# A diffusion layer on one Trainium2 core: the right-hand blocks of the second tokens made in another order, and three of them ranked lower

## The chip, the core and the metric

The kernel runs on one core of a Trainium2 chip. The metric is the device time of one execution in microseconds (us); for the kernel before it is the median of three executions, 2676.26 us (2675.55 to 2680.1). Five engines work side by side and meet through semaphores: TensorE (PE in the profile; its weight loads are PEld), VectorE (DVE), ScalarE (ACT), GpSimd (POOL) and SyncE (SP), whose queue issues most DMAs.

## The reference

The layer takes 1024 latent tokens and 256 context tokens of width 1024. Cut to what matters here:

```python
def swiglu(h, w_in, w_out):
    a, b = jnp.split(h @ w_in, 2, axis=-1)
    return (jax.nn.silu(a) * b) @ w_out
...
# 1. half-step: x += 0.5 * gate * swiglu(modulate(rms_norm(x)))       (D_FF = 2816)
# 2. mixers:    p = modulate(rms_norm(x)) @ w_in                       (1024 x 6656)
#               conv branch and attention branch from p, gated, merged, one projection
# 3. half-step: as 1, with weights of its own, then a final rms_norm
```

Everything is float32. The change touches the two large products h @ w_in of the mixers and of the second half step, and of these only the blocks made from h.

## The kernel before, in words

**Products.** The latent tokens are worked on transposed (channels on partitions), in two chunks of 512: C0, the first tokens, and C1, the second tokens. A float32 factor is held as two parts, hi (rounded to the matmul's type) and lo (the rest). `split` makes them: a cast on ACT writes hi, then a subtraction on DVE writes lo (L197). One product of a weight block with a right-hand block sums 4 k-blocks of 3 matmuls each (hi x hi, hi x lo, lo x hi; `terms`, L680), so 12 matmuls of 128x128 by 128x512 into one PSUM bank. The weight's lo part is needed by every third matmul, and so is the right-hand lo part.

**Seven products instead of eight.** The class `Winograd` takes 1024 channels as two halves and two chunks of tokens as two columns: a 2x2 block product, for which it uses seven block products. Products 1 and 2 need only the first tokens (right-hand blocks r1, r2). Products 3 to 7 need blocks made from the second tokens. With f1, f2 the two channel halves of the first tokens and b1, b2 those of the second tokens, `norm1` (L556) makes, for each k of 4 blocks of 128 channels: t1 = b1 - f1 (block 5), t2 = b2 - t1 (block 6), t3 = b2 - b1 (block 7), t2 - f2 (block 4) and b2 itself (block 3). `keep(i, k, src)` (L513) takes a buffer and splits a block into its parts. So five blocks by four k are 20 splits, and 20 rows on DVE write a lo part: these are rows r3 to r7 below.

**Weights.** Per pair of weight columns (a, b), POOL forms s1 = b0 + b1, s2 = s1 - a0, s3 = a0 - b0 and, when s2 has been split, s2 again as a1 - s2. `parts` splits these on ACT and DVE into tiles `wl` (4 buffers). `lefts` (L617) lists them in the order in which they are used: s2 (product 6), s3 (product 7), b1 (product 4, from a raw tile), s1 (product 5), the second s2 (product 3).

**Stages and order.** Product results go to 5 PSUM banks. `start(norm)` (L702) runs products 1 and 2 of the first 9 pairs, one step of `norm1` after each pair's first product, so that the second tokens' blocks are made while PE has first-token products. Sums of the third pair on are put aside to DRAM. `run(norm)` ends it. Then, pair by pair, `second` (L770) uses products 6, 7 and 4 and `third` (L780) uses 5 and 3. `mix` (the mixers, `plain=True`, 9 pairs ahead) and `fast` (the second half step, 9 pairs ahead) both call `norm1()` (started at L1301 and L1776); the first half step calls it with `turned` (L1106), which takes the tokens from elsewhere.

The program is written in one order, but a scheduler that runs when the kernel is built lays out each engine's list: it ranks instructions by their place in the program, and puts on an engine the best ranked one that it reckons can run. `tc.high_priority(n)` moves the rank of what is written under it. So the order of writing, the pools and the ranks decide together which row stands where. On the chip each engine runs its list strictly in order.

**Pools.** `apool` has 38 buffers (`atile`; r blocks, h blocks, x tiles), `tpool` 11 of one 128x512 tile (`ttile`; nt, h22, s1 to s3, u, c, v, b), `wpool` 4 for `wl` and 3 for `raw`.

Of the kernel before, what the change touches and what calls it, by code (L numbers as in the profile page):

```python
# [45 lines left out]
TOKENS_AT = 5  # L46
RESIDENT, AH2, AH3 = 2, 9, 9
SLOT = 1024


@with_exitstack
def tile_dit_layer(
# [198 lines left out]
    def rstd_cols(accs, n, dim):  # L251

        nt = n // P
        pss = ps_t(nt)
        for j in range(nt):
            for i, acc in enumerate(accs):
                matmul(
                    pss[:, j : j + 1], acc[:, j * P : (j + 1) * P], ones[:], start=(i == 0),
                    stop=(i == len(accs) - 1), pinned=True,
                )  # L260
        a = small("rs_a", nt)
        dve.tensor_scalar(out=a[:], in0=pss, scalar1=dim * EPS, scalar2=None, op0=ALU.add)
# [228 lines left out]
    class Winograd:  # L491
# [61 lines left out]
                dve.tensor_add(out=accs[0], in0=accs[0], in1=sq)  # L553
            self.n_squares[ch] = n + 1

        def norm1(self, turned=None):  # L556

            if turned is None:
                y = rstd_cols(self.accs[C1], 512, D)
                yield  # L560
                pr = bcast(y, 512)
                yield
            t12, t22 = {}, {}

            def scaled(k):
                t22[k] = ttile("h22")
# [5 lines left out]
                for t, i in ((t12[k], k), (t22[k], k + 4)):  # L572
                    if turned is not None:
                        self.shifted(t, i, turned(i))
                        continue
                    dve.tensor_mul(out=t, in0=self.xs(i, C1), in1=pr)
                    self.shifted(t, i)

            scaled(0)
            for k in range(4):  # L580
                f, b12, b22 = self.h0[k], t12[k], t22[k]
                t1, t2, t3 = ttile("nt"), ttile("nt"), ttile("nt")
                dve.tensor_sub(out=t1, in0=b12, in1=f[:, 0])
                self.keep(3, k, b22)
                dve.tensor_sub(out=t3, in0=b22, in1=b12)
                if k < 3:
                    scaled(k + 1)
                dve.tensor_sub(out=t2, in0=b22, in1=t1)
                self.keep(7, k, t3)
                self.keep(5, k, t1)  # L590
                self.keep(6, k, t2)
                dve.tensor_sub(out=t2, in0=t2, in1=f[:, 1])
                self.keep(4, k, t2)
                yield
# [1268 lines left out]
```

## Time and profile before

| | |
|---|---|
| median of three executions | 2676.26 us (2675.55 to 2680.1) |
| the profiled execution's own time | 2677.21 us |
| its span in the profile | 2675.3 us, at a mean granted clock of 0.995 |
| PE busy | 2637.8 us, 99% of the span |
| DVE busy | 2007.0 us, 75% |
| ACT, POOL busy | 1172.3 us (44%), 557.1 us (21%) |

The mixers' `start` ends near 950 us, that of the second half step near 2075 us. A page of the profile gives whole-span shares; the timeline view prints pieces of one engine with the idle time ahead of each in brackets and, behind the arrow, what ended it; the windows view gives the busy time of each engine in a stretch. All operations are recorded by one helper, so all carry line L90, and tiles tell them apart (r, wl, nt, uc with their numbers left out).

### The profile page before, as it was taken

The page shows a single profiled execution, that of the slowest core. Times are in us where ns is not written, and L with a number is a line of the kernel's source. Part 1 is how long each engine was busy: PE and PEld are TensorE (multiplying, and loading weights), DVE is VectorE, ACT ScalarE, POOL GpSimd, SP SyncE. Part 2 cuts the span into 40 slices and gives each one's busy share as a digit, 9 for nine tenths or more (in the row PEclk, how much of TensorE's full clock was granted, in tenths as well). Part 3 has the DMA queues.
Part 4 walks back from the last instruction along what each step waited for, and adds up shares of the span by engine and source line. Part 5 has one row for each costly group of instructions (what it writes and reads, how often), then busy time and mean ns, then how long its engine had stood idle before and what let it go on. Part 6 is the DMA issues. An engine that isn't in the chain of part 4 may idle for free.

```text
span 2675.3 us, 36939 instructions
## 1 busy us (share of the span) xinstructions
PE 2637.8 (99%) x13373; PEld 2222.0 (83%) x13373; DVE 2007.0 (75%) x3356; ACT 1172.3 (44%) x2317; POOL 557.1 (21%) x449
## 2 busy tenths in 40 slices
PE   8999999999999999999999999999999999999998
PEld 6787799888778878888999888888888788888888
DVE  5788976788877899877588676685458876667885
ACT  6532454333453643333355576574236333334443
POOL 0134201211010044332033122141001442320200
PEclk9999999999999999999999999999999999999999
DMA  8566475345974345332522432113524543228841
GB/s 316 196 190 191 141 227 165 108 131 197 300 188 110 114 157 173 114 126 79 201 66 94 91 95 61 35 42 99 164 87 146 181 153 93 89 87 284 189 90 64
DMA packets 369744, 376.93 MB, mean 141 GB/s; under 512 B 19334, under 2 KB 258072, under 8 KB 369560
## 3 DMA queue, kind: packets, MB, share of 16 engines
q1 hardware_dynamic: 358744, 353.03, 40.7%
q0 software_dynamic: 10816, 21.53, 4.9%
q8 instruction: 105, 1.72, 0.3%
q14 instruction: 79, 0.65, 0.1%
HBM read 306.78 MB, written 67.67 MB: 140 GB/s over the span
## 4 chain that ended last, share of the span: by engine, by line
PE 92%; DVE 4%; issue 1%; DMA 1%; ACT 1%; POOL 0%; SPq 0%; DVEq 0%; POOLq 0%; ACTq 0%
PE ps L90 76%; PE po L90 8%; PE pt L90 8%; DVE r L90 1%; DVE wl L90 1%; DVE nt L90 0%; DVE macc L90 0%; DMA rawm<-in_w_mod_dram 0%; DVE uc L90 0%; POOL s L90 0%; DMA raw<-in_ffn_w_in_dram 0%; DMA ws<-in_ffn_w_out_dram 0%; DVE v L90 0%; DVE y L90 0%; DMA mcol<-mrow 0%
## 5 line engine op out<-in xcount | busy, mean ns | idle before, releaser
L90 PE MATMUL ps<-r,wl 128*128 128x512 f32 x5196 | 1206.9, 391 | 10.6 <-DVE wl L90 5.2
L90 PEld LDWEIGHTS ps<-r,wl 128*128 128x128 f32 x5196 | 973.6, 188 | 220.1 <-DVE wl L90 7.7
L90 ACT CAST wl<-s 128x512 fp32r<-128x512 f32 x254 | 156.8, 620 | 322.2 <-PE ps L90 225.1
L90 POOL TENSOR_TENSOR s<-raw 128x512 f32<-128x512 f32 x64 | 91.9, 1436 | 891.3 <-DMA raw<-in_ffn_w_in_dram 583.5
L90 ACT CAST wl<-raw 128x512 fp32r<-128x512 f32 x287 | 177.5, 620 | 219.1 <-PE ps L90 157.6
L90 DVE TENSOR_TENSOR wl<-raw,wl 128x512 fp32r<-128x512 f32 x287 | 202.4, 706 | 62.5 <-ACT wl L90 59.7
L90 DVE TENSOR_TENSOR wl<-s,wl 128x512 fp32r<-128x512 f32 x254 | 230.7, 909 | 18.3 <-ACT wl L90 16.9
L90 POOL TENSOR_TENSOR s<-raw,s 128x512 f32<-128x512 f32 x64 | 103.9, 1624 | 363.2 <-DVE wl L90 363.2
L90 DVE SCALAR_TENSOR_TENSOR macc<-rawm,silu_c,macc 128x512 f32<-128x512 f32 x178 | 149.7, 858 | 12.5 <-DMA rawm<-in_w_mod_dram 11.7
L90 PE MATMUL ps<-wh,r 128*128 128x256 f32 x768 | 141.6, 284 | 0.0
L90 DVE TENSOR_TENSOR u<-u,ps 128x512 f32<-128x512 f32 x174 | 118.3, 680 | 29.0 <-PE ps L90 28.9
L90 DVE TENSOR_TENSOR pts<-pt,pts 128x512 fp32r<-128x512 f32 x160 | 108.7, 687 | 40.8 <-ACT pts L90 39.0
L90 ACT CAST pts<-pt 128x512 fp32r<-128x512 f32 x160 | 93.3, 595 | 86.5 <-PE pt L90 82.6
L90 ACT CAST rh<-hid 128x512 fp32r<-128x512 f32 x132 | 81.3, 620 | 109.5 <-PE ps L90 94.5
L90 DVE TENSOR_REDUCE m<-ps 128x1 f32<-128x512 f32 (+1 forms) x192 | 110.3, 595 | 24.1 <-PE ps L90 20.4
L90 PE MATMUL ps<-rh,wl 128*128 128x512 f32 x360 | 123.1, 392 | 2.8 <-ACT rh L90 2.8
L90 PEld LDWEIGHTS ps<-wh,r 128*128 128x128 f32 x768 | 120.8, 192 | 0.7 <-issue 0.6
L90 ACT CAST wh<-raw 128x512 fp32r<-128x512 f32 (+1 forms) x85 | 67.9, 801 | 102.1 <-PE ps L90 71.8
L90 PE MATMUL po<-pts,vh 128*128 128x512 f32 x256 | 110.0, 435 | 0.2 <-ACT pts L90 0.2
L90 PE MATMUL ps<-wl,r 128*128 128x256 f32 x384 | 109.0, 284 | 0.0
L90 DVE TENSOR_TENSOR rl<-hid,rh 128x512 fp32r<-128x512 f32 x132 | 90.1, 686 | 22.8 <-PE ps L90 13.4
L90 PE MATMUL ps<-kl,qs 128*128 128x512 f32 x384 | 104.2, 395 | 0.0
(314 smaller groups left out, 5117.4 us busy)
## 6 DMA issues: line engine op xcount, KB each, us to landing
raw<-in_ffn_w_in_dram SPq DMA_DIRECT2D x130, 512.0 KB
raw<-in_ffn_w_out_dram SPq DMA_DIRECT2D x72, 512.0 KB
raw<-in_w_in_dram SPq DMA_DIRECT2D x61, 512.0 KB
rawm<-in_w_mod_dram SPq DMA_DIRECT2D x104, 256.0 KB
hid<-hd SPq DMA_DIRECT2D x40, 512.0 KB
rawm<-in_w_mod_dram SPq DMA_DIRECT2D x32, 512.0 KB
ws<-in_ffn_w_out_dram POOLq DMA_DIRECT2D x30, 512.0 KB, 6.5
ucd<-uc SPq DMA_DIRECT2D x25, 512.0 KB
```

What stands on the lines that cost most here:

```text
L90: inst = getattr(self.engine, name)(*args, **kw)
```

## The change

`norm1` is written anew for the mixers and the second half step, and its old order stays as `norm1_turned` for the first half step, which is thereby unchanged. In the new `norm1` each step makes blocks 6 and 7 of its k, and only the float32 sources of blocks 5, 3 and 4. These sources stand in six `apool` buffers named `raws` (two k in one) where t1 and b2 stood in `ttile`s before. After the fourth k the blocks 4, 5 and 3 are split, four k each, all under a rank 300 lower. The operations and their number are the same: DVE has 3265 rows before and after, with 20 splits per stage.

```diff
+LATER = 300
...
+        def norm1(self):
...
+            def raw(i, k):
+                if k % 2 == 0:
+                    held[i] = atile("raws", (P, 2, 512))
+                raws[i, k] = held[i][:, k % 2]
+                return raws[i, k]
...
+                for t, i in ((t12[k], k), (raw(3, k), k + 4)):
                     dve.tensor_mul(out=t, in0=self.xs(i, C1), in1=pr)
                     self.shifted(t, i)
+
+            scaled(0)
+            for k in range(4):
+                f, b12, b22 = self.h0[k], t12[k], raws[3, k]
+                t1, t2, t3 = raw(5, k), ttile("nt"), ttile("nt")
+                dve.tensor_sub(out=t1, in0=b12, in1=f[:, 0])
+                if k < 3:
+                    scaled(k + 1)
+                dve.tensor_sub(out=t2, in0=b22, in1=t1)
+                dve.tensor_sub(out=t3, in0=b22, in1=b12)
+                self.keep(6, k, t2)
+                self.keep(7, k, t3)
+                dve.tensor_sub(out=raw(4, k), in0=t2, in1=f[:, 1])
+                if k < 3:
+                    yield
+            for i in (4, 5, 3):
+                with tc.high_priority(-LATER):
+                    for k in range(4):
+                        self.keep(i, k, raws[i, k])
+                yield
+
+        def norm1_turned(self, turned):
...
-    norm1 = half1.norm1(lambda k: turned(t1, k, ps_t if k < 4 else ps_o))
+    norm1 = half1.norm1_turned(lambda k: turned(t1, k, ps_t if k < 4 else ps_o))
```

The order of rows differs from before only around the ends of the two stages. In the rows below a name's first number counts tiles, so r4_1549 is block 4; `h22` and `nt` are the float32 sources before, `raws` those of the change; lines read L90 before and L91 after, since one line was added above.

**Mixers, DVE, before**, where the weights of the first pair's products 6, 7 and 4 (wl_1584, wl_1588, wl_1590) are split:

```order
L90 TENSOR_TENSOR nt_1541_8572<-nt_1541_8572,x1_1191_6610 128x512
L90 TENSOR_TENSOR wl_1584_8748<-s2_1582_8743,wl_1584_8748 128x512
L90 TENSOR_TENSOR r4_1549_8596<-nt_1541_8572,r4_1549_8596 128x512
L90 TENSOR_TENSOR r3_1560_8642<-h22_1544_8579,r3_1560_8642 128x512
L90 TENSOR_TENSOR r7_1561_8647<-nt_1559_8640,r7_1561_8647 128x512
L90 TENSOR_TENSOR r5_1562_8650<-nt_1557_8638,r5_1562_8650 128x512
L90 TENSOR_TENSOR r6_1563_8653<-nt_1558_8639,r6_1563_8653 128x512
L90 TENSOR_TENSOR wl_1588_8768<-s3_1583_8744,wl_1588_8768 128x512
L90 TENSOR_TENSOR wl_1590_8785<-raw_1580_8740,wl_1590_8785 128x512
```

**The same place with the change**; the weights of products 6 and 7 are wl_1582 and wl_1586 here:

```order
L91 TENSOR_TENSOR r4_1551_8622<-raws_1512_8454,r4_1551_8622 128x512
L91 TENSOR_TENSOR wl_1582_8746<-s2_1580_8741,wl_1582_8746 128x512
L91 TENSOR_TENSOR r4_1552_8625<-raws_1512_8454,r4_1552_8625 128x512
L91 TENSOR_TENSOR r4_1553_8628<-raws_1539_8569,r4_1553_8628 128x512
L91 TENSOR_TENSOR r4_1554_8631<-raws_1539_8569,r4_1554_8631 128x512
L91 TENSOR_TENSOR r5_1562_8673<-raws_1506_8437,r5_1562_8673 128x512
L91 TENSOR_TENSOR wl_1586_8766<-s3_1581_8742,wl_1586_8766 128x512
```

and further on (three more rows of r5, two of r3 and a sum stand between the two pieces) the weight of product 4, wl_1588:

```order
L91 TENSOR_TENSOR r3_1575_8730<-raws_1523_8499,r3_1575_8730 128x512
L91 TENSOR_TENSOR r3_1576_8733<-raws_1523_8499,r3_1576_8733 128x512
L91 TENSOR_TENSOR uc_1585_8765<-uc_1585_8765,ps_1589_8786 128x512
L91 TENSOR_TENSOR wl_1588_8783<-raw_1578_8738,wl_1588_8783 128x512
L91 TENSOR_TENSOR wl_1600_8813<-s1_1579_8740,wl_1600_8813 128x512
L91 TENSOR_TENSOR wl_1602_8831<-s2_1580_8741,wl_1602_8831 128x512
```

The lo part of product 6's weight moves from the 1187th row of the list to the 1182nd. That of product 4's stood 7 rows behind it and now stands 15 behind it, and eleven of the rows between are held-back blocks, r4_1552 to r3_1576.

**Mixers, PE, before**, from product 6 of the first pair on (x3 is all three matmuls of one k; x2 two matmuls on the weight's hi part):

```order
L90 MATMUL ps_1603_8818<-r6_1514_8458,wl_1584_8748 128x512 x3
L90 MATMUL ps_1603_8818<-r6_1531_8525,wl_1584_8748 128x512 x3
L90 MATMUL ps_1603_8818<-r6_1548_8592,wl_1584_8748 128x512 x3
L90 MATMUL ps_1603_8818<-r6_1563_8653,wl_1584_8748 128x512
L90 MATMUL ps_1605_8836<-r7_1512_8452,wl_1588_8768 128x512 x2
L90 MATMUL ps_1612_8863<-r4_1515_8462,wl_1590_8785 128x512 x2
L90 MATMUL ps_1603_8818<-r6_1563_8653,wl_1584_8748 128x512 x2
L90 MATMUL ps_1614_8880<-r5_1513_8455,wl_1602_8815 128x512 x2
```

**PE with the change**, from the last groups of product 7 on:

```order
L91 MATMUL ps_1603_8834<-r7_1538_8566,wl_1586_8766 128x512 x3
L91 MATMUL ps_1603_8834<-r7_1550_8618,wl_1586_8766 128x512 x3
L91 MATMUL ps_1610_8861<-r4_1551_8622,wl_1588_8783 128x512 x2
L91 MATMUL ps_1612_8878<-r5_1562_8673,wl_1600_8813 128x512 x2
L91 MATMUL ps_1614_8896<-r3_1573_8724,wl_1602_8831 128x512 x2
L91 MATMUL ps_1610_8861<-r4_1551_8622,wl_1588_8783 128x512
L91 MATMUL ps_1610_8861<-r4_1552_8625,wl_1588_8783 128x512 x3
L91 MATMUL ps_1610_8861<-r4_1553_8628,wl_1588_8783 128x512 x3
```

Products 6 and 7 run through whole. Then PE takes, of each of products 4, 5 and 3, the two matmuls on the weight's hi part, and its next one needs the lo part of wl_1588.

**Second half step, DVE, before**; the weights of products 6, 7 and 4 are wl_3619, wl_3623 and wl_3625:

```order
L90 TENSOR_TENSOR r7_3581_19451<-nt_3577_19438,r7_3581_19451 128x512
L90 TENSOR_TENSOR r5_3582_19454<-nt_3575_19436,r5_3582_19454 128x512
L90 TENSOR_TENSOR r6_3583_19457<-nt_3576_19437,r6_3583_19457 128x512
L90 TENSOR_TENSOR wl_3619_19613<-s2_3617_19608,wl_3619_19613 128x512
L90 TENSOR_TENSOR wl_3623_19633<-s3_3618_19609,wl_3623_19633 128x512
L90 TENSOR_TENSOR nt_3576_19437<-nt_3576_19437,h0_3478_18939 128x512
L90 TENSOR_TENSOR wl_3625_19650<-raw_3615_19605,wl_3625_19650 128x512
L90 TENSOR_TENSOR uc_3622_19632<-uc_3622_19632,ps_3626_19653 128x512
L90 TENSOR_TENSOR wl_3630_19671<-s1_3616_19607,wl_3630_19671 128x512
L90 TENSOR_TENSOR r4_3584_19461<-nt_3576_19437,r4_3584_19461 128x512
```

**With the change**; they are wl_3615, wl_3619 and wl_3621:

```order
L91 TENSOR_TENSOR r5_3596_19539<-raws_3539_19300,r5_3596_19539 128x512
L91 TENSOR_TENSOR uc_3603_19569<-uc_3603_19569,ps_3616_19612 128x512
L91 TENSOR_TENSOR r5_3597_19542<-raws_3566_19415,r5_3597_19542 128x512
L91 TENSOR_TENSOR r5_3598_19545<-raws_3566_19415,r5_3598_19545 128x512
L91 TENSOR_TENSOR wl_3615_19609<-s2_3613_19604,wl_3615_19609 128x512
L91 TENSOR_TENSOR wl_3619_19629<-s3_3614_19605,wl_3619_19629 128x512
L91 TENSOR_TENSOR r3_3606_19587<-raws_3538_19295,r3_3606_19587 128x512
L91 TENSOR_TENSOR wl_3621_19646<-raw_3611_19601,wl_3621_19646 128x512
L91 TENSOR_TENSOR r3_3607_19590<-raws_3538_19295,r3_3607_19590 128x512
L91 TENSOR_TENSOR uc_3618_19628<-uc_3618_19628,ps_3622_19649 128x512
L91 TENSOR_TENSOR r3_3608_19593<-raws_3556_19362,r3_3608_19593 128x512
L91 TENSOR_TENSOR wl_3626_19667<-s1_3612_19603,wl_3626_19667 128x512
```

Blocks 4 and 5 are done before the weights of product 6; product 6's lo part moves from the 2605th row to the 2609th. The last rows of block 3 stand between the weights' rows.

**Second half step, PE, before**, the end of the first pair's products:

```order
L90 MATMUL ps_3631_19674<-r6_3598_19518,wl_3619_19613 128x512 x2
L90 MATMUL ps_3640_19719<-r4_3599_19522,wl_3625_19650 128x512 x3
L90 MATMUL ps_3644_19757<-r3_3544_19306,wl_3632_19689 128x512 x3
L90 MATMUL ps_3644_19757<-r3_3561_19373,wl_3632_19689 128x512 x3
L90 MATMUL ps_3644_19757<-r3_3578_19440,wl_3632_19689 128x512 x3
L90 MATMUL ps_3644_19757<-r3_3595_19507,wl_3632_19689 128x512 x3
L90 MATMUL ps_3650_19783<-r6_3549_19323,wl_3639_19716 128x512 x2
```

**PE with the change**, the beginning of the first pair's second products:

```order
L91 MATMUL ps_3627_19670<-r6_3543_19311,wl_3615_19609 128x512 x2
L91 MATMUL ps_3629_19688<-r7_3544_19314,wl_3619_19629 128x512 x2
L91 MATMUL ps_3636_19715<-r4_3584_19485,wl_3621_19646 128x512 x2
L91 MATMUL ps_3638_19735<-r5_3595_19536,wl_3626_19667 128x512 x2
L91 MATMUL ps_3627_19670<-r6_3543_19311,wl_3615_19609 128x512
L91 MATMUL ps_3627_19670<-r6_3557_19369,wl_3615_19609 128x512 x3
```

Before, the last group of product 4 needed r4_3599, DVE's 2617th row. With the change the last row that product 3 needs is r3_3609, also the 2617th; product 6's lo part is the first that PE comes to, behind 8 matmuls on weights' hi parts.

More of the change, by code (lines that the diff above doesn't have):

```diff
@@ L554, in square @@
             self.n_squares[ch] = n + 1
[L556 to L563, printed above, removed]
+        def norm1(self):
+            y = rstd_cols(self.accs[C1], 512, D)
+            yield
+            pr = bcast(y, 512)
+            yield
+            t12, raws, held = {}, {}, {}
+            def raw(i, k):
[3 more added lines that the diff above has]
+                return raws[i, k]
             def scaled(k):
-                t22[k] = ttile("h22")
                 if self.plain:
@@ L571, in scaled @@
                     t12[k] = ttile("h12")
[L572 to L575, printed above, removed]
+                for t, i in ((t12[k], k), (raw(3, k), k + 4)):
                     dve.tensor_mul(out=t, in0=self.xs(i, C1), in1=pr)
                     self.shifted(t, i)
+            scaled(0)
[11 more added lines that the diff above has]
+                if k < 3:
+                    yield
+            for i in (4, 5, 3):
+                with tc.high_priority(-LATER):
+                    for k in range(4):
+                        self.keep(i, k, raws[i, k])
+                yield
+        def norm1_turned(self, turned):
+            t12, t22 = {}, {}
+            def scaled(k):
+                t22[k], t12[k] = ttile("h22"), ttile("h12")
+                for t, i in ((t12[k], k), (t22[k], k + 4)):
+                    self.shifted(t, i, turned(i))
             scaled(0)
```

## The prediction

> **What bounds the kernel now.** I read the page's shares and its chain first, then PE's timeline around the ends of the two stages that call `norm1`, then what DVE, POOL, SP and ACT do there. From the page, busy time by engine and the chain's shares:
>
> ```profile
> PE 2637.8 (99%) x13373; PEld 2222.0 (83%) x13373; DVE 2007.0 (75%) x3356; ACT 1172.3 (44%) x2317; POOL 557.1 (21%) x449
> ...
> PE 92%; DVE 4%; issue 1%; DMA 1%; ACT 1%; POOL 0%; SPq 0%; DVEq 0%; POOLq 0%; ACTq 0%
> ```
>
> PE is busy for 99% of the span. No matmul goes or comes, so the change can only touch what PE waits. PE's timeline (start, us, engine, group; in brackets the idle time ahead and what ended it) in the mixers, then in the second half step:
>
> ```profile
> 922.01 30.87 PE L90 MATMUL ps<-r,wl 128*128 128x512 f32 x135
> 955.67 1.89 PE L90 MATMUL ps<-r,wl 128*128 128x512 f32 x7 [2.79 <-DVE wl L90]
> 957.80 1.77 PE L90 MATMUL ps<-r,wl 128*128 128x512 f32 x5 [0.24 <-ACT r L90]
> 959.96 18.66 PE L90 MATMUL ps<-r,wl 128*128 128x512 f32 x81 [0.38 <-DVE r L90]
> ```
>
> ```profile
> 2031.29 43.73 PE L90 MATMUL ps<-r,wl 128*128 128x512 f32 x191
> 2075.24 0.73 PE L90 MATMUL ps<-r,wl 128*128 128x512 f32 x2 [0.22 <-DVE r L90]
> 2077.57 0.50 PE L90 MATMUL ps<-r,wl 128*128 128x512 f32 x1 [1.61 <-ACT r L90]
> 2078.30 4.37 PE L90 MATMUL ps<-r,wl 128*128 128x512 f32 x18 [0.23 <-DVE r L90]
> 2083.54 31.82 PE L90 MATMUL ps<-r,wl 128*128 128x512 f32 x139 [0.86 <-DVE wl L90]
> ```
>
> The waits are 2.79 + 0.24 + 0.38 = 3.41 us in the mixers and 0.22 + 1.61 + 0.23 + 0.86 = 2.92 us in the second half step, 6.33 us in all or 0.24% of the time. That is the most that a better order can give, and each of them ends on a row of DVE or of ACT that makes parts. Why they are late, the windows show (length; busy us and count of PE, PEld, DVE, ACT, POOL; granted clock; DMA share; GB/s):
>
> ```profile
> 950.00:960.00 10.00, 6.56 (x26) 4.12 (x24) 9.92 (x15) 5.37 (x10) 2.11 (x2) 1.00 0.26 96
> 2060.00:2070.00 10.00, 10.00 (x45) 8.09 (x44) 9.39 (x11) 4.79 (x10) 5.72 (x4) 1.00 0.36 120
> 2070.00:2080.00 10.00, 7.94 (x33) 5.72 (x32) 9.25 (x10) 3.71 (x7) 4.71 (x3) 1.00 0.55 186
> ```
>
> DVE is full in both places, 9.92 and 9.39 of 10 us. So DVE is the local bound: a row moved ahead there pushes others back, one for one.
>
> **The units.** A long piece of the chain gives PE's time per matmul; DVE's timeline, from a row to a later one, gives DVE's:
>
> ```profile
> 1040.37 117.11 PE ps L90 x516
> ```
>
> ```profile
> 2031.57 1.28 DVE L90 TENSOR_TENSOR h<-x,pt 128x512 f32<-128x512 f32 x2 [0.42 <-PE pt L90]
> ...
> 2059.22 0.68 DVE L90 TENSOR_TENSOR r<-h,r 128x512 fp32r<-128x512 f32 x1
> 2060.61 0.69 DVE L90 TENSOR_TENSOR uc<-uc,ps 128x512 f32<-128x512 f32 x1 [0.71 <-PE ps L90]
> 2061.22 4.06 DVE L90 TENSOR_TENSOR r<-nt,r 128x512 fp32r<-128x512 f32 x3
> 2065.20 1.28 DVE L90 TENSOR_TENSOR wl<-s,wl 128x512 fp32r<-128x512 f32 x2
> ```
>
> A matmul costs 117.11 / 516 = 0.227 us. The first and the second of these DVE rows are 46 places apart in its list, so a row costs (2059.22 - 2031.57) / 46 = 0.60 us when nothing disturbs it.
>
> **Mixers, what goes.** DVE's timeline here, with the rows on which the argument rests:
>
> ```profile
> 951.93 0.68 DVE L90 TENSOR_TENSOR nt<-h,h 128x512 f32<-128x512 f32 x1
> ...
> 954.94 0.68 DVE L90 TENSOR_TENSOR wl<-s,wl 128x512 fp32r<-128x512 f32 x1
> ...
> 958.02 1.88 DVE L90 TENSOR_TENSOR r<-nt,r 128x512 fp32r<-128x512 f32 x3
> ...
> 962.41 1.61 DVE L90 TENSOR_TENSOR r<-nt,r 128x512 fp32r<-128x512 f32 x1
> ```
>
> The row at 954.94 writes the lo part of product 6's weight and is what the 2.79 us wait ends on; it is the 1187th of DVE's list, and the row at 951.93 is the 1182nd. The new list has product 6's lo part there. It is then done by 952.6, before PE comes at 922.01 + 30.87 = 952.88, and the wait goes. The two small waits for r rows go too: blocks 6 and 7 all stand ahead.
>
> **Mixers, what comes.** Products 6 and 7 hold 24 matmuls, then PE has 2 each of products 4, 5 and 3 that use the weight's hi part only: 30 in all, until 952.88 + 30 x 0.227 = 959.7. Next it needs the lo part of product 4's weight, which now stands 15 rows behind that of product 6. Fifteen rows from 951.93 on end at 962.41 in the trace, so this part would start there and be written by 963.1: **a wait of 3.4 us**. The 15 rows at 0.60 us would take only 9.0 and leave 1.9. More is possible, because POOL moves ahead as well. POOL's timeline, and SP's queue:
>
> ```profile
> 955.70 1.85 POOL L90 TENSOR_TENSOR s<-raw,s 128x512 f32<-128x512 f32 x1 [5.44 <-DVE wl L90]
> 961.33 2.13 POOL L90 TENSOR_TENSOR s<-raw 128x512 f32<-128x512 f32 x1 [3.78 <-DMA raw<-in_w_in_dram]
> ...
> 2058.63 2.43 POOL L90 TENSOR_TENSOR s<-raw 128x512 f32<-128x512 f32 x1 [202.95 <-DMA raw<-in_ffn_w_in_dram]
> 2061.14 1.29 POOL L90 TENSOR_TENSOR s<-s,raw 128x512 f32<-128x512 f32 x1
> 2062.39 1.74 POOL L90 TENSOR_TENSOR s<-raw,raw 128x512 f32<-128x512 f32 x1
> ```
>
> ```profile
> 957.58 3.94 SPq L90 DMA_DIRECT2D raw<-in_w_in_dram  x2
> ```
>
> POOL's last operation of the pair waits for the very lo part that moves ahead by 5 rows, 3 us. It ends at 957.55, SP issues the next pair's load at 957.58 and POOL's next three operations begin at 961.33. With the change that burst begins near 959 (3.0 us earlier would be 958.3; the load's landing may not follow wholly) and lies on the 15 rows for about 4 us. What a burst costs, the second half step shows: the three r rows at 2061.22 took 4.06 us, and the three at 958.02 took 1.88 with POOL idle, so 2.2 us were lost to a burst of 5.5 us. Four us of it are worth at most 1.6; the rows here are partly sums from PSUM, so I take 1.2. The wait then is 3.4 + 1.2 = **4.6 us, bounds 1.9 and 5.6** (3.4 and all 2.2). Against the 3.41 that goes: **+1.2 us, bounds -1.5 and +2.2**. Behind PE in this wait stand product 5's and 3's rest; their lo parts are the next two rows of DVE, so nothing further is late.
>
> **Second half step.** Here PE must wait later, not sooner. PE had done 43 of the first pair's matmuls at 2031.29 + 43.73 = 2075.02 (the 21 behind that wait are the x2, x1 and x18), so it came to product 6 at 2075.02 - 43 x 0.227 = 2065.3. In the new list 8 matmuls on hi parts come first, until 2067.1. Then PE needs the lo part of product 6's weight: it stood at 2065.20 as the 2605th row and now is the 2609th, 2065.20 + 4 x 0.60 = 2067.6, less up to 0.71 for DVE's idle time before the sum at 2060.61 (that sum now has five more rows ahead of it, so its bank is ready). Written by 2067.5 to 2068.2: a **wait of 0.4 to 1.1, taken as 0.7**. What the old waits hung on is this step of ACT and the DVE row behind it:
>
> ```profile
> 2058.57 1.66 ACT L90 CAST r<-nt 128x512 fp32r<-128x512 f32 x3
> ...
> 2076.90 0.62 ACT L90 CAST r<-nt 128x512 fp32r<-128x512 f32 x1 [5.98 <-DVE nt L90]
> ```
>
> ```profile
> 2077.55 0.69 DVE L90 TENSOR_TENSOR r<-nt,r 128x512 fp32r<-128x512 f32 x1 [0.68 <-ACT r L90]
> ```
>
> The last k of block 4 is subtracted, cast (2076.90) and subtracted again (2077.55) while PE stands. With the change block 4 lies ahead of the weights, and the last held-back row (block 3) is needed by the 60th matmul, near 2065.3 + 0.7 + 57 x 0.227 = 2078.9, and stands 8 rows behind product 6's lo part, some 2072. So these waits go. The 0.86 for the next pair's weight goes by about as much. What could bring a wait back: ACT's three r3 casts wait for buffers that DVE's block 4 and 5 rows set free, and the hi part of product 5's weight is queued behind them; three casts are 1.66 us, and PE has 1.8 us of hi parts. **-2.2 us, bounds 0 and -2.9.** SP's queue differs in the mixers only: one context load stands ahead of a weight's load, and neither is what PE waits for there.
>
> **Sum.** +1.2 - 2.2 = **-1.0 us**. On the profiled execution's own 2677.21 us (span 2675.3 and 1.9 around it) that is 2676.2; its time stands 0.95 above the median of the three, so the median would be 2675.3. Bounds by the terms: -4.4 to +2.2.
>
> **One price more: the clock.** Windows of one grid of 3.41 us (same columns):
>
> ```profile
> 29.13:32.54 3.41, 1.85 (x8) 1.20 (x9) 3.41 (x6) 1.92 (x3) 0.00 (x0) 1.00 1.11 327
> 32.54:35.95 3.41, 3.41 (x11) 2.75 (x11) 3.41 (x7) 2.54 (x5) 0.00 (x0) 0.50 1.05 400
> 742.51:745.93 3.42, 1.13 (x4) 0.67 (x4) 3.31 (x7) 3.42 (x7) 0.00 (x0) 1.00 0.98 336
> 745.93:749.34 3.41, 3.41 (x9) 2.73 (x9) 3.41 (x6) 2.80 (x6) 1.21 (x1) 0.50 1.03 309
> 954.14:957.55 3.41, 1.88 (x7) 1.24 (x7) 3.33 (x5) 2.50 (x5) 1.85 (x1) 1.00 0.37 154
> 2073.71:2077.13 3.42, 2.04 (x8) 1.05 (x6) 3.13 (x2) 0.23 (x1) 2.61 (x2) 1.00 0.49 190
> ```
>
> Behind windows with PE busy 1.85 and 1.13 us the next one ran at a granted clock of 0.50: 9 matmuls in 3.41 us at 745.93 where 15 fit, so about 1.7 us lost. The window at 954.14, with 1.88, had no such successor, and neither had the one at 2073.71: the old stalls escaped it in this execution by little, since the 2.79 us lay across the border at 954.14. A wait of 4.6 us in one piece leaves some window of such a grid with at most 1.1 us busy, wherever the grid lies, and pays. I leave this price out of the sum, because an escape by 0.03 us says that the old wait pays too in most executions, if the grid lies differently each time; that it doesn't cancel is a rival below. The Trainium skill ("TensorE: Matmul & The Clock Gate", section "What's actually happening") says of the mechanism that the gate's window is 4096 cycles, 3413 ns, and runs freely, not from the kernel's start. By that rule the borders fall elsewhere in each execution, and the sum stands as it is; the trace agrees so far as its borders 32.54, 745.93 and 954.14 are whole multiples of 3.413 us apart.
>
> **Rivals.**
> - **All the waits go**: -6.3 us, 2669.9. For it: the last held-back row is needed late, and the weights could come first. Against it: DVE is full (9.92 of 10), and eleven held-back rows stand ahead of product 4's weight.
> - **Slower: the wait at product 4 empties a clock window.** At its upper bound, 5.6 us, it costs 2.2 more than what goes, and the halved window, where the old wait escaped one as in the profiled execution, another 1.7: +3.9 in the mixers, -2.2 in the second half step, +1.7 in all: 2678.0. It decides when product 4's lo part on DVE is written after about 963.6 (a wait of 3.9, which with 1.7 uses up 3.41 and 2.2).
> - **Nothing shows**: held-back rows and weights change places on a full DVE, and the waits only change names: 0, 2676.3. For it: every row on both lists is there, at the same 0.60 us.
>
> **How the numbers follow.** Forecast 0.45; all waits gone 0.08; the clock window 0.30; nothing shows 0.17. The range goes from -4.4 (both terms at their best, 2671.9) to +3.2 (the mixers' worst, the window's 1.7, two thirds of the second step's gain lost: 2.2 + 1.7 - 0.7 = 3.2, 2679.5): 2671.5 to 2679.5. About 0.2%, 5.4 us, is what a measurement of this kernel can tell from no change. Faster by more needs nearly the whole 6.33: 0.06. Slower by more needs the worst of every term and a wait that I don't see: 0.09. Within: 0.85.
>
> **What would show it.** In PE's timeline of the changed kernel: no wait ahead of product 6 in the mixers, and one of 2 to 5.6 us some 30 matmuls later, ended by a DVE wl row; POOL's next s row near 959; in the second half step a wait under 1.2 us ahead of product 6 and none on ACT's r rows. The prediction is wrong if a wait ends on an r row of blocks 4, 5 or 3, if PE waits for a load, or if PE's pieces outside these two places change.

## The result and the profile after

The changed kernel takes **2684.84 us** (median of 11 executions, 2679.18 to 2689.36), the kernel before 2676.98 us (median of 11, 2674.68 to 2681.3). The ratio is 1.0028 with a 95% interval of 1.002 to 1.0035: **slower by 5.4 to 9.4 us**, where 1 us faster was forecast, within 2671.5 to 2679.5. From the page of the changed kernel, whose profiled execution has a span of 2681.5 us:

```profile
PE 2640.4 (98%) x13373; PEld 2224.1 (83%) x13373; DVE 2005.3 (75%) x3356; ACT 1173.6 (44%) x2317; POOL 561.5 (21%) x449
```

DVE and ACT do what they did (2007.0 and 1172.3 before), POOL's rows take 4 us more, and PE is busy 2.6 us longer with as many matmuls. So the loss is in waits and in a slower clock. PE's timeline of the change, at the same two places as in the prediction, the mixers and then the second half step:

```profile
921.16 30.87 PE L91 MATMUL ps<-r,wl 128*128 128x512 f32 x135
952.83 3.02 PE L91 MATMUL ps<-r,wl 128*128 128x512 f32 x12 [0.79 <-DVE wl L91]
956.94 3.92 PE L91 MATMUL ps<-r,wl 128*128 128x512 f32 x16 [1.09 <-DVE wl L91]
963.43 16.20 PE L91 MATMUL ps<-r,wl 128*128 128x512 f32 x63 [2.57 <-DVE wl L91]
```

```profile
2032.88 33.82 PE L91 MATMUL ps<-r,wl 128*128 128x512 f32 x148
2068.04 0.74 PE L91 MATMUL ps<-r,wl 128*128 128x512 f32 x2 [1.34 <-ACT wl L91]
2069.73 0.73 PE L91 MATMUL ps<-r,wl 128*128 128x512 f32 x2 [0.95 <-ACT wl L91]
2071.25 1.22 PE L91 MATMUL ps<-r,wl 128*128 128x512 f32 x2 [0.79 <-ACT wl L91]
2072.81 52.56 PE L91 MATMUL ps<-r,wl 128*128 128x512 f32 x221 [0.34 <-ACT wl L91]
```

The mixers wait 0.79 + 1.09 + 2.57 = 4.45 us (3.41 before). The second half step waits 1.34 + 0.95 + 0.79 + 0.34 = 3.42 us (2.92 before), now close together and all on ACT's casts of the first pair's weights. The windows view (PE busy first, the granted clock ahead of the DMA share) shows what stands behind these waits:

```profile
961.31:964.72 3.41, 1.29 (x6) 1.05 (x6) 3.41 (x4) 0.17 (x1) 3.33 (x3) 1.00 0.42 158
964.72:968.13 3.41, 3.41 (x10) 2.67 (x9) 3.41 (x5) 1.46 (x4) 1.58 (x2) 0.50 0.54 154
2067.23:2070.64 3.41, 1.47 (x4) 0.59 (x4) 3.13 (x3) 2.20 (x5) 2.78 (x3) 1.00 0.01 1
2070.64:2074.05 3.41, 2.46 (x5) 1.56 (x6) 3.41 (x6) 2.64 (x6) 0.29 (x1) 0.50 0.51 150
2074.05:2077.47 3.42, 3.42 (x9) 2.68 (x9) 2.72 (x3) 0.00 (x0) 2.69 (x2) 0.50 0.89 257
```

Windows with PE busy 1.29 and 1.47 us are followed by one window at half clock in the mixers and two in the second half step. A halved window costs 1.7 us when PE fills it. The first profile of before had none at either place. At these two places of all twenty profiles, windows at full clock with PE busy up to 1.70 us were followed by a halved one, and those with 1.75 us or more were not. A halved window with up to 2.71 us busy was followed by another, and one with 2.83 us or more was not. So the second halved window goes with the small waits inside the window at 2070.64 (2.46 us busy). Why are ACT's casts late? POOL's, DVE's and ACT's timelines of the change in the second half step:

```profile
2059.63 6.03 POOL L91 TENSOR_TENSOR s<-raw 128x512 f32<-128x512 f32 x1 [202.36 <-DMA raw<-in_ffn_w_in_dram]
2065.74 1.60 POOL L91 TENSOR_TENSOR s<-s,raw 128x512 f32<-128x512 f32 x1
2067.30 1.72 POOL L91 TENSOR_TENSOR s<-raw,raw 128x512 f32<-128x512 f32 x1
```

```profile
2059.00 0.68 DVE L91 TENSOR_TENSOR r<-nt,r 128x512 fp32r<-128x512 f32 x1
2059.61 0.68 DVE L91 TENSOR_TENSOR wl<-raw,wl 128x512 fp32r<-128x512 f32 x1
2060.21 0.68 DVE L91 TENSOR_TENSOR r<-nt,r 128x512 fp32r<-128x512 f32 x1
2060.81 3.69 DVE L91 TENSOR_TENSOR r<-raws,r 128x512 fp32r<-128x512 f32 x6
2064.42 0.68 DVE L91 TENSOR_TENSOR uc<-uc,ps 128x512 f32<-128x512 f32 x1
2065.02 2.87 DVE L91 TENSOR_TENSOR r<-raws,r 128x512 fp32r<-128x512 f32 x2
```

```profile
2067.37 0.62 ACT L91 CAST wl<-s 128x512 fp32r<-128x512 f32 x1 [5.11 <-POOL s L91]
```

POOL's first sum, s1, took 6.03 us where it took 2.43 before. It ended at 2065.66, and that is 1.24 us after DVE began its sum from a PSUM bank at 2064.42. Ahead of that row DVE ran nine rows without a break, the six r rows of blocks 4 and 5 last, each with both inputs in SBUF, where the tiles stand. So POOL stood from 2059.63 until DVE did a row that does not need two SBUF inputs, then needed 1.24 us. s2 was ready at 2067.34 (2062.43 before), and the cast of product 6's weight followed at once. Before, it was DVE's own wait that let POOL in: after the row at 2059.22 DVE stood for 0.71 us, and POOL's sum ended at 2061.06, 1.16 us after that wait began at 2059.90. The new list fills this gap with rows.

In the mixers, too, POOL's first sum of the first pair was late. Before, then with the change:

```profile
944.69 1.47 POOL L90 TENSOR_TENSOR s<-raw 128x512 f32<-128x512 f32 x1 [123.48 <-DMA raw<-in_w_in_dram]
```

```profile
944.14 4.07 POOL L91 TENSOR_TENSOR s<-raw 128x512 f32<-128x512 f32 x1 [124.14 <-DVE raws L91]
```

It ended at 948.21, 1.23 us after DVE began a sum from PSUM at 946.98, with four rows of two SBUF inputs ahead of that.

**Theory A**, then: a run of DVE rows with two SBUF inputs keeps POOL out; the weights come late; PE waits in few, close pieces; and the window behind runs at half clock. **Theory B**: only the places of rows in DVE's list count. **Theory C**: the six `raws` buffers hold something up.

To put the cost in its place, the start of a matmul in a profile is set against the same numbered matmul of the first profile of before. What is lost or gained between matmuls 4600 and 5250 is put down to the mixers, between 10500 and 10750 to the second half step.

### The profile page after: what moved, and what is told of

It reads as the page before. It is cut to its first block, busy times and chain, and to the rows that moved or that the text cites. A ratio compares the mean times of both kernels' runs of the same rounds, so it can differ in the third digit from the quotient of the medians.

```text
span 2681.5 us, 36944 instructions
## 1 busy us (share of the span) xinstructions
PE 2640.4 (98%) x13373; PEld 2224.1 (83%) x13373; DVE 2005.3 (75%) x3356; ACT 1173.6 (44%) x2317; POOL 561.5 (21%) x449
## 4 chain that ended last, share of the span: by engine, by line
PE 57%; DMA 1%; ACT 1%; DVE 0%; issue 0%; POOL 0%; DVEq 0%; POOLq 0%; ACTq 0%
PE ps L91 47%; PE pt L91 5%; PE po L91 5%; DMA y<-yd 0%; DMA raw<-in_ffn_w_in_dram 0%; DVE wl L91 0%; DVE pts L91 0%; ACT pts L91 0%; DVE m L91 0%; ACT q L91 0%; ACT pl L91 0%; POOL s L91 0%; ACT pc L91 0%; ACT wc L91 0%; ACT wl L91 0%
## 5 line engine op out<-in xcount | busy, mean ns | idle before, releaser
L91 PE MATMUL ps<-r,wl 128*128 128x512 f32 x5196 | 1207.3, 391 | 12.6 <-DVE wl L91 6.2
L91 PEld LDWEIGHTS ps<-r,wl 128*128 128x128 f32 x5196 | 974.0, 189 | 222.1 <-ACT wl L91 9.2
L91 ACT CAST wl<-s 128x512 fp32r<-128x512 f32 x254 | 157.0, 620 | 333.5 <-PE ps L91 237.0
L91 POOL TENSOR_TENSOR s<-raw 128x512 f32<-128x512 f32 x64 | 99.4, 1554 | 892.8 <-DMA raw<-in_ffn_w_in_dram 362.2
L91 ACT CAST wl<-raw 128x512 fp32r<-128x512 f32 x287 | 177.6, 620 | 227.0 <-PE ps L91 164.9
L91 DVE TENSOR_TENSOR wl<-s,wl 128x512 fp32r<-128x512 f32 x254 | 234.4, 924 | 20.1 <-ACT wl L91 18.5
L91 DVE TENSOR_TENSOR wl<-raw,wl 128x512 fp32r<-128x512 f32 x287 | 202.3, 706 | 61.0 <-ACT wl L91 58.0
L91 POOL TENSOR_TENSOR s<-raw,s 128x512 f32<-128x512 f32 x64 | 101.6, 1588 | 360.4 <-DVE wl L91 360.4
L91 DVE SCALAR_TENSOR_TENSOR macc<-rawm,silu_c,macc 128x512 f32<-128x512 f32 x178 | 150.1, 860 | 18.1 <-DMA rawm<-in_w_mod_dram 17.1
L91 PE MATMUL ps<-wh,r 128*128 128x256 f32 x768 | 141.6, 284 | 0.0
L91 DVE TENSOR_TENSOR pts<-pt,pts 128x512 fp32r<-128x512 f32 x160 | 108.6, 686 | 41.1 <-ACT pts L91 39.1
L91 DVE TENSOR_TENSOR u<-u,ps 128x512 f32<-128x512 f32 x174 | 118.1, 679 | 27.3 <-PE ps L91 27.1
L91 ACT CAST pts<-pt 128x512 fp32r<-128x512 f32 x160 | 93.2, 595 | 86.3 <-PE pt L91 82.2
L91 ACT CAST rh<-hid 128x512 fp32r<-128x512 f32 x132 | 81.3, 620 | 109.7 <-PE ps L91 93.5
L91 DVE TENSOR_REDUCE m<-ps 128x1 f32<-128x512 f32 (+1 forms) x192 | 110.2, 594 | 23.9 <-PE ps L91 22.4
L91 PE MATMUL ps<-rh,wl 128*128 128x512 f32 x360 | 124.1, 395 | 2.8 <-ACT rh L91 2.8
L91 PEld LDWEIGHTS ps<-wh,r 128*128 128x128 f32 x768 | 120.8, 192 | 0.7 <-issue 0.6
L91 ACT CAST wh<-raw 128x512 fp32r<-128x512 f32 (+1 forms) x85 | 67.9, 801 | 101.6 <-PE ps L91 74.1
L91 PE MATMUL po<-pts,vh 128*128 128x512 f32 x256 | 109.9, 435 | 0.2 <-ACT pts L91 0.2
L91 PE MATMUL ps<-wl,r 128*128 128x256 f32 x384 | 109.0, 284 | 0.0
L91 DVE TENSOR_TENSOR rl<-hid,rh 128x512 fp32r<-128x512 f32 x132 | 89.8, 684 | 22.4 <-PE ps L91 13.6
L91 PE MATMUL ps<-kl,qs 128*128 128x512 f32 x384 | 104.3, 395 | 0.6 <-ACT pc L91 0.6
```

Source lines behind the costliest of these rows:

```text
L91: inst = getattr(self.engine, name)(*args, **kw)
```

## The experiments

| run | ratio to before (95%) | mixers, us | second half step, us |
|---|---|---|---|
| the change | 1.0028 (1.002 to 1.0035) | +1.7 | +3.0 |
| e1 only mixers | 1.0013 (1.0004 to 1.0021) | +1.4 | 0.0 |
| e2 only second half step | 1.0009 (1.0001 to 1.0018) | +2.1 | +3.0 |
| e3 small rows | 1.0028 (1.0019 to 1.0037) | +4.9 | -1.9 |
| e4 small rows, both | 1.0023 (1.0013 to 1.0033) | +3.3 | -0.2 |
| e5 e2 and 2 small rows | 1.0011 (1.0002 to 1.0021) | +0.4 | -1.9 |
| e6 weights first | 0.9991 (0.9982 to 1.0) | +0.4 | -2.8 |
| e7 raws, old order | 1.0004 (0.9996 to 1.0013) | +3.3 | -1.5 |
| e8 e6 and small rows | 1.0017 (1.0008 to 1.0025) | +2.1 | -1.9 |
| e9 no rank | 1.0021 (1.0012 to 1.0031) | +3.2 | +2.8 |
| e16 e6 and one small row | 1.0008 (0.9997 to 1.0019) | -0.7 | -3.0 |
| e17 e16 without a new tile | 0.9993 (0.9984 to 1.0002) | -0.5 | -3.0 |
| e18 e5 without a new tile | 0.9996 (0.9987 to 1.0004) | +0.1 | -2.0 |
| change again (e10, e12, e13, e14) | one execution each | +1.7, +4.3, +4.1, +4.4 | +2.8, +2.5, +2.8, +3.1 |
| before again (e11, e15) | one execution each | +1.4, +0.4 | 0.0, -0.7 |

**e1 and e2: one stage each.** The old `norm1` is kept beside the new one as `norm1_old`.

```diff
-    fast.start(fast.norm1())
+    fast.start(fast.norm1_old())        # e1; in e2 mix.norm1_old() instead
```

> The new order in the mixers alone, the second half step as before. Theory A (POOL is kept from its sums by runs of DVE rows that read two SBUF inputs, the weights' parts come late, PE waits in one piece and the window behind runs at half clock): PE waits about 4.4 us around the first pair's products as with the change (before 3.41), one halved window there, none of the change's waits in the second half step; 2 to 3.5 us slower than before. Theory B (only the places of rows in DVE's list count, POOL and clock don't): about 1 us slower. Theory C (the six raws buffers hold up loads everywhere): waits for DMA appear, 3 us or more.

> The new order in the second half step alone, the mixers as before. A: POOL's first s row takes about 6 us as with the change, PE's waits there are about 3.4 us and end on ACT wl, one or two halved windows; 3 to 5 us slower than before, and with the run of the mixers alone about the whole of the change's 7.5. B: 2 us faster than before, as was forecast from the rows.

The ratios add up to 1.0022, near the change's 1.0028. Each stage shows its own waits again, 4.40 us in e1's mixers and 3.41 us in e2's second half step with POOL's first sum at 5.73 us. B's gain of 2 us in the second half step didn't come. e2's mixers, with the old list, paid two halved windows behind the old 2.79 us wait (+2.1); the first profile of before had paid none.

**e3 and e4: small rows to let POOL in.**

```diff
+            act.copy(out=t[:, 0], in_=src)
+            dve.reduce_max(out=gap[:, i : i + 1], in_=t[:, 0, :64].bitcast(F32), axis=AX.X)
+            dve.tensor_sub(out=t[:, 1], in0=src, in1=t[:, 0].bitcast(F32))
```

> The change, with a small DVE row (a maximum over 64 columns of the hi part just written, one SBUF input) ahead of each held-back lo row, 12 per stage: more DVE work, and the same operations otherwise. In the second half step the first of these stands at the head of the run of r4 and r5 rows. A: POOL gets in at it, its first s row takes under 3 us instead of 6.03, PE's waits there fall from 3.4 to under 1.5 us, and the kernel is 2 to 5 us faster than the change; the mixers stay as they are, since POOL's long row there ends before the first of these rows. B: 12 more rows on a full DVE, 0 to 2 us slower than the change, POOL's row still about 6 us or the wait unchanged.

> As the run with small rows, and small rows also ahead of the lo rows of blocks 6 and 7 of the last two k, so that POOL can get in earlier in the mixers too. A: POOL's first s row in the mixers takes under 2.5 us instead of 4.07, the weight of product 6 comes before PE needs it, waits there under 3 us; 1 to 3 us faster still, near the kernel before or below it. B: slower than the change by 1 to 3 us.

In the second half step A held: e3's first sum took 2.85 us, PE waited 1.36 us and no window there was halved, 5 us better than the change. The whole was no faster, against what A expected: the mixers had 6.4 us of waits and two halved windows, and all was 4 us later before the mixers began (see e17). Waits of 6.4 us lie inside the change's own spread there (4.4 to 7.1 us, see e10 to e15), so that the twelve more rows made the mixers worse isn't shown. e4 missed too: POOL's first sum in the mixers fell to 2.79 us (4.07 in the change), and then an r row came late, with a wait of 3.51 us.

**e5 and e18: two small rows, in the second half step alone**, ahead of the first row of blocks 4 and 5; mixers as before. In e5 the maximum goes to a new constant tile, in e18 to a column of `cols` that nothing reads any more. The row in which the two differ (e5 also allocates the tile), shortened:

```diff
-                        dve.reduce_max(out=gap[:, i : i + 1], ...)   # e5
+                        dve.reduce_max(out=cols[:, :1], ...)         # e18
```

> Mixers as before; the second half step with the new order and two small DVE rows, ahead of the first held-back row of block 4 and the first of block 5. Theory A (POOL kept out by runs of two-input DVE rows): POOL's first s row takes under 3.5 us there instead of 5.7 to 6, PE waits 1 to 1.5 us in place of 3.4 and no window behind is halved; 2 to 4 us faster than the new order in the second half step alone, within 1.5 us of before or below it. Theory B (only the count of DVE rows ahead of a weight's row): no faster than the new order in the second half step alone (2.5 to 3.5 us above before).

> The mixers as before and the second half step with the new order and two small rows, again without a new tile. If the tile did it: 2 to 4 us faster than with the tile (2681.1), so 2677 to 2679, within 1.5 us of before and 2 to 4 us faster than the new order in the second half step alone, as theory A said of the small rows there. If not: about 2681 again.

DVE's, POOL's and PE's timelines of e18:

```profile
2062.87 0.22 DVE L91 TENSOR_REDUCE cols<-r 128x1 f32<-128x64 f32 x1
2063.00 6.86 DVE L91 TENSOR_TENSOR r<-raws,r 128x512 fp32r<-128x512 f32 x6
```

```profile
2061.85 2.26 POOL L91 TENSOR_TENSOR s<-raw 128x512 f32<-128x512 f32 x1 [202.50 <-DVE r L91]
2064.19 1.62 POOL L91 TENSOR_TENSOR s<-s,raw 128x512 f32<-128x512 f32 x1
2065.78 1.73 POOL L91 TENSOR_TENSOR s<-raw,raw 128x512 f32<-128x512 f32 x1
```

```profile
2071.30 0.73 PE L91 MATMUL ps<-r,wl 128*128 128x512 f32 x2 [0.82 <-ACT wl L91]
2072.45 22.78 PE L91 MATMUL ps<-r,wl 128*128 128x512 f32 x99 [0.42 <-DVE wl L91]
```

One row of 0.22 us is enough: POOL's sum ends at 2064.11, 1.24 us after that row began, and two more sums follow. (e5 and e3 agree: 1.25 and 1.23 us after their first small row.) Now DVE's six rows take 6.86 us instead of 3.69, because the two engines take turns: singly, the rows take 1.66, 1.78 and 1.77 us, one to each of POOL's three sums, and then 0.68 us each. PE waits 1.24 us, in place of 3.41 with two halved windows: -2.0 us against +3.0 in e2, with the same new order. That settles the second half step for A against B. e5's trace says the same (waits of 0.83 and 0.42 us), but its time missed what A expected: 1.0011, no better than e2's 1.0009 (for the likely reason see e17).

**e6 and e9: the lists of the mixers.** e6 takes the rank away, writes blocks 5 and 3 behind the first pair's weights and keeps that order on ACT and DVE; e9 only takes the rank away. e6's edit, shortened:

```diff
-                with tc.high_priority(-LATER):
-                    for k in range(4):
-                        self.keep(i, k, raws[i, k])
-                yield
+                strict[0] = i in (5, 3)
+                for k in range(4):
+                    self.keep(i, k, raws[i, k])
+                strict[0] = False
+                for _ in range(4 if i == 4 else 1):
+                    yield
...
-                yield parts(s2)
+                yield parts(s2, j == 0 and not side_from)    # s3 and b[1] too: kept in order
```

> The change, with blocks 5 and 3 kept behind the weights of the first pair's products 6, 7 and 4 on ACT and DVE (they are written behind them and keep that order; no rank). The weight of product 4 has 3 DVE rows between it and product 6's in place of 14, and in the second half step 4 instead of 8 held-back rows stand ahead of product 6's. Theory A: in the mixers the wait of 2.6 us at product 4 goes, the 0.8 us ahead of product 6 stays (POOL's first row still about 4 us, since the rows that keep it out are of blocks 6, 7 and 4); in the second half step POOL gets in 1.2 us sooner and PE waits 2 to 2.5 us instead of 3.4; 3 to 5 us faster than the change. A rival, that the held-back blocks then come late: waits that end on an r row of blocks 5 or 3, no faster than the change.

> The change without its rank (LATER = 0). The second half step's list is the same there; in the mixers product 7's weight moves behind blocks 5 and 3 (8 rows later), product 6's two rows later. Theory A and B alike: the second half step's waits stay at 3.4 us, the mixers wait longer (product 7's weight about 4 us later, but product 4's as before): 0 to 3 us slower than the change. If the rank itself cost the time, it is faster than the change.

In e6 the three waits of the mixers' first products became 0.29, 0.27 and 1.46 us (the last one now at product 5), none followed by a halved window, and in the second half step 0.52 and 0.27. e6 is as fast as before or faster, 8 us better than the change, so the change's loss is one of order and not of the new buffers, which e6 has too. e9's mixers waited 2.00 + 1.69 + 0.64 us, and two windows were halved. The rank alone was thus not the cause of the loss: without it the kernel is 1.0021.

**e7: the buffers alone**, as an edit of the kernel before:

```diff
-                t1, t2, t3 = ttile("nt"), ttile("nt"), ttile("nt")
+                t1, t2, t3 = raw(5, k), ttile("nt"), ttile("nt")     # h22 and block 4's source likewise
```

> The old order of splits, with the sources of blocks 5, 3 and 4 in six buffers of the large pool as in the change, instead of the small pool. Theory C (the buffers do it): 2 us or more of the change's 7.5 appear here, as waits for loads or for buffers. Theory A and B: within 1.5 us of before.

1.0004: C falls, as PE got no wait on a load in the two stages. The buffers still alter the scheduler's order: e7 has one wait of 4.88 us in the mixers, ended by ACT's cast of a weight, which costs as much there as the change does (+3.3), and less in the second half step.

**e8, e16 and e17: weights first, with small rows.** e8 has one ahead of block 4's first row in both stages and one ahead of block 6's third in the mixers, e16 only the former, e17 is e16 without the new tile.

> The kernel with the weights ahead of blocks 5 and 3, and one small DVE row per stage ahead of block 4's first lo row and, in the mixers, one ahead of block 6's third. Theory A: POOL's first s row takes under 3 us in both stages (4.07 and 6.03 in the change), PE's waits in the two stages sum to under 3.5 us (before 6.33, the change 7.9), and no window behind them is halved; 1 to 4 us faster than before. Theory B: no difference from the run without the small rows.

> The kernel with the weights ahead of blocks 5 and 3, and one small DVE row per stage ahead of block 4's first lo row, none in the mixers' earlier rows. Theory A: POOL's first s row in the second half step takes under 3 us (4.68 without the small row), PE waits there 0.8 us or less, and the mixers are as without it; the whole within 1 us of the run without small rows, 0 to 4 us faster than before. If the small row costs more than it brings, the second half step waits longer than 0.8 us.

> The run with the weights ahead and one small row per stage, with the small row's result written to a column that nothing reads any more instead of a new constant tile, so that no buffer of the kernel moves; the lists are the same otherwise. The five runs with a new tile stand 3.1 to 4.5 us later at the 2400th matmul, before any changed row. If the new tile did that, this run stands within 2 us of before there and comes out 2 to 4 us faster than with the tile (2675 to 2677), 0 to 3 us faster than before. If it was chance, about 2679 again.

e8 missed: its row in the mixers cost more than it brought (a wait of 3.19 us on an r row, two halved windows), and its profile has a wait of 3.76 us in the output products that nothing here explains. e17's timeline of PE:

```profile
952.93 0.73 PE L92 MATMUL ps<-r,wl 128*128 128x512 f32 x2 [0.28 <-ACT wl L92]
953.93 8.76 PE L92 MATMUL ps<-r,wl 128*128 128x512 f32 x36 [0.27 <-ACT wl L92]
964.15 15.98 PE L92 MATMUL ps<-r,wl 128*128 128x512 f32 x69 [1.46 <-DVE wl L92]
```

```profile
2030.74 47.63 PE L92 MATMUL ps<-r,wl 128*128 128x512 f32 x209
2079.23 15.96 PE L92 MATMUL ps<-r,wl 128*128 128x512 f32 x69 [0.86 <-DVE wl L92]
```

Its median is 2674.94 us against 2677.89 (0.9993, 0.9984 to 1.0002): 10 us better than the change, not proven faster than before. e16 was expected within 1 us of e6 and came out 2.7 us above it. The new tile may be why: the profiles of all five runs with it (e3, e4, e5, e8, e16) stood 3.1 to 4.5 us later than before's at matmul 2400, ahead of any changed row. The other fifteen stand between -2.7 and +2.6, with e17 and e18, which have the lists of e16 and (but for the place of one small row) of e5, at 0.6 and 1.8. The medians of e17 and e18 are 4.1 and 4.8 us lower than those of e16 and e5, though the intervals of the ratios overlap. So the tile's cost is likely, but not shown, and by what a tile of 48 bytes a partition or less would do that was not tried.

**e10 to e15: the two kernels again.**

> The change once more, for its profile. If the waits are set by the lists and the ports, they come out as before to 0.2 us (4.4 us in the mixers, 3.4 us in the second half step), and only the number of halved windows behind them differs, 1 or 2 at each place, by where the grid of 3.413 us windows lies. If they are chance, the waits themselves differ by 1 us or more.

> The change a third time, for the same question: waits of 4.4 and 3.4 us to 0.2 us, one or two halved windows at each place.

> The change a fourth time. Theory A: the second half step waits 3.0 to 3.5 us with two halved windows, as in each of the three profiles so far; the mixers wait either 4.4 us (the second pair's load lands while DVE's r3 rows hold POOL off) or 6.9 us (it lands before them and DVE's three r3 rows take 4.8 us instead of 1.9). If the mixers' wait takes other values, something else decides it.

> The change a fifth time, for the same: 4.4 or 6.9 us in the mixers, 3.0 to 3.5 us in the second half step.

> The kernel before once more, for its profile: waits of 3.4 and 2.9 us again; behind the 2.8 us one in the mixers a halved window unless the wait lies across a border of the grid, and in the second half step none or one. The stages then cost 0 to 3.4 us more than in the first profile, which had no halved window at either.

> Before a third time: 2.8 to 3.4 us of waits in the mixers with none, one or two halved windows behind, 2.9 us in the second half step with none, since its waits are in pieces.

In the second half step the waits of five profiles of the change agree to 0.5 us, with two halved windows in each; before has none there in three profiles. In the mixers the wait at product 4 has two values, 2.57 us (first profile, e10) and 5.00, 5.22, 5.20 (e12, e13, e14); e12 was expected at the first value. Behind the old order's wait there, before had no halved window in its first profile and one each in e11 and e15. DVE's and POOL's timelines of e10, then of e12:

```profile
965.57 1.88 DVE L91 TENSOR_TENSOR r<-raws,r 128x512 fp32r<-128x512 f32 x3
```

```profile
965.62 2.96 POOL L91 TENSOR_TENSOR s<-raw 128x512 f32<-128x512 f32 x1 [5.33 <-DMA raw<-in_w_in_dram]
```

```profile
962.54 4.79 DVE L91 TENSOR_TENSOR r<-raws,r 128x512 fp32r<-128x512 f32 x3
```

```profile
962.16 1.29 POOL L91 TENSOR_TENSOR s<-raw 128x512 f32<-128x512 f32 x1 [4.90 <-DMA raw<-in_w_in_dram]
```

In e10 the second pair's load landed 0.05 us after DVE began its three r3 rows: they took 1.88 us and POOL waited. In e12 it landed 0.38 us before them: POOL did its three sums, the r3 rows took 4.79 us, and the weight of product 4, behind them in DVE's list, came 2.4 us later. In e13 and e14 too the load landed before those rows, while DVE's sum from PSUM ran. It is a race, decided by when a load lands.

## Why the prediction was wrong, point by point

- **"The mixers' wait goes and comes back at product 4"**: the place was right. Its size was 2.57 us in two of five profiles and 5.0 to 5.2 us in three, against 4.6 forecast with bounds of 1.9 and 5.6. Wrong was that products 6 and 7 would not wait: 0.79 and 1.09 us stayed. POOL's first sum took 4.07 us instead of 1.47; that this made products 6 and 7 wait is argued from the trace and not shown by a run. Six profiles with the new list (the five and e1) give +3.0 us on the average, six with the old list +0.7 (before, e2, e5, e11, e15, e18). So the stage cost 2.2 us where 1.2 was forecast.
- **"Second half step: -2.2 us, bounds 0 and -2.9"**: this step failed. It counted DVE rows ahead of product 6's low part and took s2 as ready when it was before. The held-back rows in front made a long run of two-input rows, POOL's sum took 6.03 us instead of 2.43, and the wait came from ACT, ahead of any DVE row. It measured +0.5 us of waits and 2.4 us more by the halved windows, 2.9 us in all (mean of the five profiles and e2); with the old list four profiles lie between -0.7 and 0.0. The prediction even named DVE's idle 0.71 us as time that the new list saves; it was the gap through which POOL had got in. The prediction had seen what POOL takes from DVE (the 4.06 us for three rows), and not that DVE takes as much from POOL.
- **"I leave this price out of the sum"**: the reason held in the mixers, where the old wait too pays in most executions (halved windows behind it in e2, e5, e11, e15 and e18, none in the first profile). It did not hold in the second half step: there the old waits lie in pieces and paid in none of four profiles, and the new ones paid twice in all six. The rival with the clock window was the nearest of the three: its longer wait at product 4 came in three of five profiles, but it kept the gain of 2.2 us in the second half step, where the larger part of the loss lies.
- **The sum**: 2.2 in the mixers and 2.9 + 0.2 in the second half step make 5.3 us, at the low end of the interval of 5.4 to 9.4. Some 2 us up to its middle are not placed. One more halved window near 2657 us, behind short matmuls, is in all five profiles of the change, but also in two of three of before, and in none of e6, e7, e16 and e17; its cause was not tried.
- **The signs named**: the wait behind 28 matmuls of the first products came as said, ended by a DVE wl row, and no wait in the second half step ended on ACT's r rows. "No wait ahead of product 6" and "under 1.2 us" were false, and so the forecast; POOL's next s row began at 960.20, not near 959.

By the Trainium skill ("SBUF — State Buffer", section "Who interferes with whom") a DVE instruction with two SBUF inputs and a GpSimd instruction that reads SBUF contend for a port, and the one that issues first holds the other off wholly. The runs agree that one holds the other off: 1.24 us from DVE's first other row to POOL's end, in the change (2064.42 to 2065.66) and in e18 (2062.87 to 2064.11). They don't bear out that the one that issues first always goes first: in the second half step POOL's sum was passed by seven DVE rows that began after it. At most other places it was not passed. In the change's profile 37 sums began, after a pause of POOL, under a DVE row of two SBUF inputs with another right behind it, and 32 of them got in ahead of that next row. So did the pair's last sum in the mixers, in the midst of r rows (four took 3.59 us, and 2.49 undisturbed):

```profile
952.70 3.59 DVE L91 TENSOR_TENSOR r<-raws,r 128x512 fp32r<-128x512 f32 x4
```

```profile
952.85 1.68 POOL L91 TENSOR_TENSOR s<-raw,s 128x512 f32<-128x512 f32 x1 [1.23 <-DVE wl L91]
```

What makes DVE keep POOL out at one place and yield at another was not tried and stays open.

## What to carry to other kernels

Before DVE rows are put one behind another, look for what POOL is to do at that time: a run of rows with two SBUF inputs can hold POOL off for the run's whole length (it did at the two places where it mattered here), and a single short row without them let it in. A wait of PE is worth more than its length when it stands in one piece or in pieces close together, as the next window may run at half clock, so compare what each window is left with and not the sums. The lower rank left fourteen rows between the weights of products 6 and 4 in the mixers; a kept order (e6) left three.

## What the runs showed of the hardware that was not expected

- Once let in, POOL and DVE took turns: POOL's three sums each held up one of DVE's next six rows (1.66, 1.78 and 1.77 us in place of 0.68, e18). Where POOL wasn't yet in, seven or more rows of the same kind passed it (the change, e2).
- At the two places a window of 3.41 us was followed by one at half clock when PE was busy for 1.70 us of it or less, and a halved window by another when PE was busy for 2.71 us or less. Elsewhere the limit can lie otherwise: a window of before with 1.85 us busy (29.13) was followed by a halved one too.
- 0.4 us in the landing of a load decide between a wait of 2.6 and one of 5.0 to 5.2 us (e10 against e12).
- A constant tile that touches no list came with about 4 us before the first changed row (e5 against e18, e16 against e17); that it is the cause isn't shown.
